# A gated delta-rule layer on one core: causal masks multiplied in on VectorE, in place of ScalarE copies and GpSimd masks

## The chip, the core and the metric

The kernel runs on one core of one Trainium2 chip. The metric is the device time of one execution in microseconds (us), as the median of several runs. The engines are named as the profile names them: PE is TensorE's matmul, PEld its weight load, DVE is VectorE, ACT is ScalarE, POOL is GpSimd, and SP is the engine that issues nearly all DMAs. Each engine works through its own instructions in a fixed order and stops at an instruction whose inputs are not there.

## The reference, cut to what matters

One layer (SEQ 2048, D_MODEL 1024) has an RWKV-7 time mixer with 12 heads of 64, a memory cross-attention beside it, an output projection and a squared-ReLU MLP. The time mixer's state update runs token by token:

```python
def step(S, inp):
    r_t, w_t, k_t, v_t, a_t, b_t = inp
    sa = jnp.einsum('bhvk,bhk->bhv', S, a_t)
    S = (S * w_t[:, :, None, :] + sa[..., None] * b_t[:, :, None, :]
         + v_t[..., None] * k_t[:, :, None, :])
    return S, jnp.einsum('bhvk,bhk->bhv', S, r_t)
```

Within a chunk of 64 tokens this becomes products of all tokens with all tokens (b and k against a and r), of which only the part with the source before the target token counts. For a that is strictly before, for r it includes the token itself. The masks of this case set the other part to zero.

## The kernel before

The program has three parts in time. First the input is normed and the first quarter of the input projection is made (0 to about 218 us). Then comes the scan: 16 pairs of two 64-token chunks, each with `prepare(p)`, `scan` and `post`, while the remaining projections, the memory attention and the output projection are laid between the scan's steps as filler (218 to about 1520 us). Last comes the MLP in four long stretches of matmuls (1520 us to the end).

The order on each engine is made by the framework's scheduler, from priorities: `dense` spreads the filler's steps over given stretches of pairs, and the first half of `prepare` is moved forward by `UPS = 400` ranks, so that it lies beside the scan of the pair before. The scheduler places each instruction where its own model of time lets it run, so an edit in one place moves instructions around it.

The change is in `prepare`, at the products within a chunk. For each chunk and each half `hb` of the heads, 6 matmuls (L390, shown as 12 in the profile, since each is two passes) write two PSUM tiles `pps` of 128x384. The tiles come from the pool `psa`, which has two buffers under the tag "a". So the next group of products can start only when both are copied out. The copies (L392) put them into the SBUF tile `PT`. Then two DMAs (L395) store the two 32x32 diagonal blocks to DRAM (`nd`). Ti is loaded from `nd` (L412), and a forward substitution of 46 + 46 dependent small DVE operations runs on it (`zt`, L431, and `Zw`, L435). Its result goes through DRAM (`zdr`) into `Z`; DVE transposes blocks of Z (`te`, L453), PE multiplies them with `PT` (L459), and the scan then uses `PT` and `Z` (L485 and on). The masks (L397, on GpSimd) work in place on `PT` behind the two stores: 64 rows by 12x64, then 64 rows by 12x128, for each chunk.

Other names below: `psco` (L772) are the memory attention's scores, `pout` (L629) the output projection, `wo` (L92 and L93) its weights split into a high and a low part, `sl` (L676) the token shift, `qt` (L756) the square of the memory attention's queries behind a load.

Of the kernel before, what the change touches and what calls it, by code (L numbers as in the profile page):

```python
# [13 lines left out]
ALU = mybir.AluOpType  # L14
# [5 lines left out]
P = 128  # L20
# [6 lines left out]
NB = MW // P  # L27
NH = 12
# [5 lines left out]
C = 64  # L34
# [26 lines left out]
def hybrid_layer(  # L61
# [6 lines left out]
    nc = tc.nc  # L68
# [129 lines left out]
    K = {}  # L198
# [82 lines left out]
    def prepare(p):  # L281
# [98 lines left out]
        for c in range(2):  # L380
            d = ch[c]
            d["PT"] = PT = ck.tile([P, NH, 2 * C], F32, name="PT", bufs=4)
            for hb in range(2):

                pps = [psa.tile([P, 3, 2 * C], F32, tag="a", name="pp") for _ in range(2)]
                for j in range(3):
                    b = 3 * hb + j
                    for q in range(2):
                        rs = slice(q * HD, q * HD + HD)
                        nc.tensor.matmul(pps[q][:, j, :], BK[c][rs, b, :], d["AR"][rs, b, :], start=True, stop=True)  # L390
                for q in range(2):
                    nc.scalar.copy(PT[:, q * NB + 3 * hb : q * NB + 3 * hb + 3, :], pps[q])  # L392
            for blk in range(2):
                bsl = slice(32 * blk, 32 * blk + 32)
                nc.sync.dma_start(nd[blk, c].rearrange("i s t -> s i t"), PT[bsl, :, bsl])  # L395
            for o, w in ((0, C), (C, 0)):
                nc.gpsimd.tensor_tensor(PT[o : o + C, :, w:], PT[o : o + C, :, w:],  # L397
                                        K["msk"][o : o + C, w:].unsqueeze(1).to_broadcast([C, NH, 2 * C - w]),
                                        op=ALU.mult)
        nc.vector.tensor_tensor(kp, kp, R, op=ALU.mult)  # L400
        psb = psz.tile([P, NH], F32, tag="z", name="psb")
        for b in range(NB):
# [24 lines left out]
        for s in range(31):  # L427
# [6 lines left out]
            for j0, j1 in parts:  # L434
                nc.vector.tensor_tensor(Zw[:, j0:j1, s + 1 :], Zw[:, j0:j1, s + 1 :], zt[:, j0:j1, :nt],  # L435
                                        op=ALU.add)
# [408 lines left out]
    S = scan_setup()  # L845
    rank["base"] = tc.cur_priority
    nxt = prepare(0)
    dense(*SPAN[0], (project(1), 184))
    dense(*SPAN[1], (mixed(project(2), memory(0), 184, 24), 208))
    dense(*SPAN[2], (mixed(project(3), memory(1, 2), 184, 48), 232))  # L850
    for p in range(NPAIR):
        d = nxt
        S, states = scan(d, S)
        if p + 1 < NPAIR:
            nxt = prepare(p + 1)
        post(p, d, states)
        if p == 3:
            dense(*SPAN[3], (mixed(output(0), memory(3), 64, 24), 88))
        elif p in (7, 11):
            dense(*SPAN[p // 4 + 3], (output(p // 4), 64))  # L860
        elif p in (13, 15):
            dense(*SPAN[p // 2], (output(3, (p // 2 % 2,)), 32))
# [104 lines left out]
    def layer1(hf, B):  # L967
# [14 lines left out]
        def w(src, name):  # L982
# [3 lines left out]
            return h, l  # L986

        nxt = prepare(0)
        for c in range(NCH):
            A, (S1, S2, S3, S4) = nxt  # L990
# [150 lines left out]
```

## Time and profile before

| what | value |
|---|---|
| median of 3 runs | 2778.41 us (2771.92 to 2782.58) |
| the profiled execution | 2781.47 us, of which its span is 2779.8 us |
| PE busy | 2620.1 us (94%), granted clock 0.956 on average |
| DVE, ACT, POOL busy | 1807.5, 1410.8, 413.1 us |

PE is busy for most of the span, so the time is read from PE: where it waits, and at which clock it works. The granted clock is a share of full speed; the chip grants 1.2 or 2.4 GHz, so 0.5 is the lower level and 1.0 the higher.

### The profile page before, as it was taken

The numbers are of one execution on the slowest core, as the hardware profiler recorded it, in microseconds if no ns is written. First come the engines' busy times: TensorE is split into PE (matmuls) and PEld (weight loads), VectorE is DVE, ScalarE is ACT, GpSimd is POOL, SyncE is SP. The second block draws the span as 40 slices with busy tenths as digits, with TensorE's granted clock in tenths as the row PEclk, the third lists the DMA queues.
The fourth block names the chain that finished last, engine by engine and source line by source line (L and its number), as shares of the span: only waits on it lengthen the run. The fifth ranks groups of instructions, "written<-read, shape, count | busy, mean of one in ns | idle before, by whom it ended". The sixth has DMA issues, their size and how long they took to land.

```text
span 2779.8 us, 49460 instructions
## 1 busy us (share of the span) xinstructions
PE 2620.1 (94%) x17620; PEld 2131.9 (77%) x17620; DVE 1807.5 (65%) x4500; ACT 1410.8 (51%) x3053; POOL 413.1 (15%) x236
## 2 busy tenths in 40 slices
PE   6989999999899998997996999999999999999999
PEld 4777777777677777777885888878888888888887
DVE  4556657676866666778568777765875666655564
ACT  5564456465645547363446444444744444544443
POOL 2002133425304241333111000000100000000000
PEclk9999999999989988798997999999999999999999
DMA  8987564665454544335574576786775444456675
GB/s 251 286 263 215 166 176 135 168 174 165 135 152 138 144 126 120 100 86 164 160 241 133 201 260 244 275 306 191 246 258 170 145 144 155 150 192 208 211 252 167
DMA packets 468444, 519.35 MB, mean 187 GB/s; under 512 B 117538, under 2 KB 291682, under 8 KB 468196
## 3 DMA queue, kind: packets, MB, share of 16 engines
q1 hardware_dynamic: 468196, 516.18, 60.0%
q8 instruction: 139, 2.28, 0.3%
q14 instruction: 109, 0.89, 0.1%
HBM read 361.86 MB, written 154.14 MB: 186 GB/s over the span
## 4 chain that ended last, share of the span: by engine, by line
PE 74%; DMA 10%; DVE 9%; ACT 2%; issue 2%; SPq 2%; POOL 1%; DVEq 0%; ACTq 0%; POOLq 0%
PE pu L964 23%; PE py L1073 22%; PE pz L102 12%; PE pout L629 5%; PE pp L390 2%; DVE zt L431 1%; DVE Zw L435 1%; DMA zdr<-Zw 1%; PE prhs L485 1%; DMA qt<-q_d 1%; DMA KT<-rk_d 1%; DMA Z<-zdr 1%; DMA xt<-in_x_dram 1%; DMA ws<-in_rw_in_dram 1%; PE py L522 1%
## 5 line engine op out<-in xcount | busy, mean ns | idle before, releaser
L102 PE MATMUL pz<-xh,w 128*128 128x512 f32 x1408 | 484.9, 413 | 4.5 <-DVE last L681 2.7
L1073 PE MATMUL py<-wpl,hhh 128*128 128x512 f32 x896 | 349.3, 390 | 0.0
L1073 PE MATMUL py<-wph,hhl 128*128 128x512 f32 x896 | 348.3, 389 | 0.0
L1073 PE MATMUL py<-wph,hhh 128*128 128x512 f32 x896 | 344.0, 391 | 0.0
L102 PEld LDWEIGHTS pz<-xh,w 128*128 128x128 f32 x1408 | 268.9, 193 | 71.8 <-issue 6.6
L93 DVE TENSOR_TENSOR hhl<-hr,hhh 128x512 fp32r<-128x512 f32 x224 | 154.7, 691 | 225.6 <-ACT hhh L92 225.5
L92 ACT CAST hhh<-hr 128x512 fp32r<-128x512 f32 x224 | 139.1, 621 | 311.1 <-PE py L1073 295.5
L102 PE MATMUL pz<-xl,w 128*128 128x512 f32 x704 | 287.7, 409 | 0.4 <-DVE xl L93 0.4
L629 PE MATMUL pout<-wo,xh 128*128 128x256 f32 x1024 | 218.7, 307 | 18.9 <-DVE wo L93 9.6
L431 DVE TENSOR_TENSOR zt<-Ti,Zw 96x96 f32<-96x96 f32 (+20 forms) x736 | 171.2, 256 | 69.3 <-DMA Ti<-nd 49.7
L397 POOL TENSOR_TENSOR PT<-PT,msk 64x768 f32<-64x768 f32 x64 | 178.6, 2790 | 131.4 <-ACT PT L392 129.1
L629 PEld LDWEIGHTS pout<-wo,xh 128*128 128x128 f32 x1024 | 174.5, 205 | 28.9 <-DVE wo L93 12.3
L1073 PEld LDWEIGHTS py<-wph,hhl 128*128 128x128 f32 x896 | 168.4, 188 | 35.0
L1073 PEld LDWEIGHTS py<-wph,hhh 128*128 128x128 f32 x896 | 168.4, 188 | 34.8 <-DVE u L999 0.2
L1073 PEld LDWEIGHTS py<-wpl,hhh 128*128 128x128 f32 x896 | 168.4, 188 | 34.6
L435 DVE TENSOR_TENSOR Zw<-Zw,zt 96x96 f32<-96x96 f32 (+20 forms) x736 | 161.2, 242 | 6.7
L102 PEld LDWEIGHTS pz<-xl,w 128*128 128x128 f32 x704 | 135.8, 193 | 29.8 <-issue 1.9
L93 DVE TENSOR_TENSOR wpl<-wr,wph 128x512 fp32r<-128x512 f32 x224 | 153.3, 684 | 3.8 <-ACT wph L92 3.8
L629 PE MATMUL pout<-wo,xl 128*128 128x256 f32 x512 | 153.1, 299 | 0.0
L86 POOL TENSOR_TENSOR nr<-nm,nhalf 128x1 f32<-128x1 f32 x34 | 28.1, 827 | 789.2 <-DVE nm L84 736.3
L92 ACT CAST wph<-wr 128x512 fp32r<-128x512 f32 x224 | 138.2, 617 | 8.5 <-PE pu L964 7.5
L390 PE MATMUL pp<-AR,BK 64*128 64x128 f32 x768 | 94.5, 322 | 18.5 <-ACT PT L392 16.3
(293 smaller groups left out, 5640.5 us busy)
## 6 DMA issues: line engine op xcount, KB each, us to landing
w<-w_d SPq DMA_DIRECT2D x264, 256.0 KB, 4.0
hr<-hc_d SPq DMA_DIRECT2D x224, 256.0 KB, 2.8
ws<-in_w_ff_dram SPq DMA_DIRECT2D x32, 1024.0 KB, 5.7
hc_d<-hs SPq DMA_DIRECT2D x128, 256.0 KB, 2.2
wr<-t_d SPq DMA_DIRECT2D x128, 256.0 KB, 3.1
wr<-in_w_ff_dram SPq DMA_DIRECT2D x96, 256.0 KB, 3.0
w_d<-w SPq DMA_DIRECT2D x88, 256.0 KB, 4.2
ws<-in_w_out_dram SPq DMA_DIRECT2D x80, 256.0 KB, 4.3
```

What stands on the lines that cost most here:

```text
L86: nc.gpsimd.tensor_tensor(t1, t0, nhalf[: ssum.shape[0], :n], op=ALU.pow)
L92: nc.scalar.copy(hi, src)
L93: nc.vector.tensor_tensor(lo, src, hi.bitcast(F32), op=ALU.subtract)
L102: nc.tensor.matmul(ps, a(k), b(k), start=(k == 0 and i == 0), stop=(k == nk - 1 and i == 2))
L390: nc.tensor.matmul(pps[q][:, j, :], BK[c][rs, b, :], d["AR"][rs, b, :], start=True, stop=True)
L397: nc.gpsimd.tensor_tensor(PT[o : o + C, :, w:], PT[o : o + C, :, w:], K["msk"][o : o + C, w:].unsqueeze(1).to_broadcast([C, NH, 2 * C - w] ...
L431: nc.vector.tensor_tensor(zt[:, j0:j1, :nt], Ti[:, s, s + 1 :].unsqueeze(1).to_broadcast([96, j1 - j0, nt]), Zw[:, j0:j1, s : s + 1].to_br ...
L435: nc.vector.tensor_tensor(Zw[:, j0:j1, s + 1 :], Zw[:, j0:j1, s + 1 :], zt[:, j0:j1, :nt], op=ALU.add)
L485: nc.tensor.matmul(pc[rs, h // 2, :], PT[:, head(h), :C], WV[:, h * HD : (h + 1) * HD], start=True, stop=True)
L629: nc.tensor.matmul(po[:, t, :], a(k, t), w[k][:, b], start=(k == 0 and i == 0 and t == 0), stop=(k == KB - 1 and i == 2 and t == 1))
L964: nc.tensor.matmul(ps, a[u][:, k * P : (k + 1) * P], b[v][:, k, :], start=(first and k == 0 and i == 0), stop=(k == 3 and i == 2), skip_gr ...
L1073: nc.tensor.matmul(ps[bk], a[u][:, m * P : (m + 1) * P], b[v], start=(fresh and c == 0 and t == 0), stop=(c == NCH - 1 and t == 2), skip_g ...
```

## The change

The ScalarE copy of each product tile becomes a VectorE multiplication with the mask, which reads the product from PSUM and the mask `msk` from SBUF and writes the masked product to `PT`. The two GpSimd operations per chunk go away. The stores to `nd` now carry masked blocks; the substitution reads only what lies above the diagonal.

```diff
                 for q in range(2):
-                    nc.scalar.copy(PT[:, q * NB + 3 * hb : q * NB + 3 * hb + 3, :], pps[q])
+                    nc.vector.tensor_tensor(PT[:, q * NB + 3 * hb : q * NB + 3 * hb + 3, :], pps[q],
+                                            K["msk"].unsqueeze(1).to_broadcast([P, 3, 2 * C]), op=ALU.mult)
             for blk in range(2):
                 bsl = slice(32 * blk, 32 * blk + 32)
                 nc.sync.dma_start(nd[blk, c].rearrange("i s t -> s i t"), PT[bsl, :, bsl])
-            for o, w in ((0, C), (C, 0)):
-                nc.gpsimd.tensor_tensor(PT[o : o + C, :, w:], PT[o : o + C, :, w:],
-                                        K["msk"][o : o + C, w:].unsqueeze(1).to_broadcast([C, NH, 2 * C - w]),
-                                        op=ALU.mult)
```

Lines behind the edit have numbers lower by 3 in the changed kernel (te is L453 before and L450 now).

The order on ACT before, at the products of the fourth pair: the copies to PT stand between other work, two of them behind `qt`, which waits for a load.

```order
L392 COPY PT<-pp 128x384 x2
L92 CAST xh<-pt 128x4x128 x3
L756 ACTIVATE qt<-qt 128x256
L392 COPY PT<-pp 128x384 x2
L92 CAST xh<-pt 128x4x128
L392 COPY PT<-pp 128x384
L150 ACTIVATE junk,nss<-xt 128x1024
L392 COPY PT<-pp 128x384 x2
L461 COPY te_2003<-pe 32x192
L470 COPY PT<-AR 64x6x64
L392 COPY PT<-pp 128x384
```

The order on DVE now, at the same place: the multiplications stand there, and six of the eight are behind the transposes `te` of the pair before, which wait for the load of Z.

```order
L84 TENSOR_SCALAR ym<-var 128x12
L392 TENSOR_TENSOR PT<-pp,msk 128x384
L349 SCALAR_TENSOR_TENSOR th_6823<-th_6845,kk 128x768
L392 TENSOR_TENSOR PT<-pp,msk 128x384
L450 STREAM_TRANSPOSE te<-Z_2000 32x192 x2
L539 SCALAR_TENSOR_TENSOR mean<-mean,yr 128x12
L350 SCALAR_TENSOR_TENSOR th_6823<-th_6823,EM 128x768
L365 TENSOR_TENSOR th_6845<-th_6845,KT 128x768
L673 SCALAR_TENSOR_TENSOR sl<-pz,muc,sl 128x511
L675 SCALAR_TENSOR_TENSOR sl<-last_149,muc,sl 128x1
L678 COPY last_150<-pz 128x1
L392 TENSOR_TENSOR PT<-pp,msk 128x384 x5
```

What moved: the emptying of the product tiles left ACT's row behind `qt` and entered DVE's row behind `te`.

The order on PE before, at the products of the last pair: all four groups stand one behind the other, with nothing between them.

```order
L522 MATMUL py_16310<-S,AR 64x64 x12
L528 MATMUL py_16310<-WV,PT 64x64 x12
L800 MATMUL po<-pT,vm 64x128 x7
L390 MATMUL pp<-AR,BK 128x128 x24
L629 MATMUL pout<-wo,xh 128x256 x3
L629 MATMUL pout<-wo,xl 128x256
```

And on PE now, from the first group of the same pair to the next rows: each group is followed by some 20 matmuls of the output projection.

```order
L390 MATMUL pp<-AR,BK 128x128 x6
L626 MATMUL pout<-wo,xh 128x256
L626 MATMUL pout<-wo,xl 128x256 x2
L626 MATMUL pout<-wo,xh 128x256 x2
L626 MATMUL pout<-wo,xl 128x256
L626 MATMUL pout<-wo,xh 128x256 x2
```

What moved: filler now lies between the groups of the last pair.

## Rows read from the trace of the kernel before

**Rows 1.** The page's busy time of each engine (share of the span, instructions).

```profile
PE 2620.1 (94%) x17620; PEld 2131.9 (77%) x17620; DVE 1807.5 (65%) x4500; ACT 1410.8 (51%) x3053; POOL 413.1 (15%) x236
```

**Rows 2.** Two stretches: length, busy by engine, clock, DMA share, GB/s.

```profile
218.00:1520.00 1302.00, 1193.65 (x11377) 971.88 (x11375) 879.66 (x2887) 684.86 (x1708) 382.72 (x191) 0.92 0.54 154
1520.00:2780.00 1260.00, 1249.72 (x5438) 1017.96 (x5438) 809.45 (x1282) 598.56 (x1027) 9.93 (x7) 0.99 0.63 208
```

**Rows 3.** Waits of PE, 218:1520: us in total, times, longest.

```profile
PE pt L936 <- DVE xn L931: 21.8, 5, 8.0
PE pp L390 <- ACT PT L392: 16.3, 7, 4.6
PE pout L629 <- DVE wo L93: 9.6, 7, 2.8
PE psco L772 <- DVE sl L676: 9.2, 1, 9.2
```

**Rows 4.** Groups, 218:1420: count, busy us, mean ns, idle before, releasers.

```profile
L397 POOL TENSOR_TENSOR PT<-PT,msk 64x768 f32<-64x768 f32 x64 | 178.6, 2790 | 131.4 <-ACT PT L392 129.1
...
L390 PE MATMUL pp<-AR,BK 64*128 64x128 f32 x768 | 94.5, 322 | 18.5 <-ACT PT L392 16.3 <-DVE BK L368 1.8 <-DVE BK L360 0.2
...
L392 ACT COPY PT<-pp 128x384 f32<-128x384 f32 x128 | 56.7, 479 | 80.8 <-PE pp L390 80.4
...
L459 PE MATMUL pe<-te,PT 32*32 32x32 f32 x768 | 38.1, 197 | 10.1 <-ACT te L461 5.6 <-DVE te L453 3.7 <-ACT BKT L419 0.7
```

**Rows 5.** Timeline of DVE, 749:764: start us, us, instruction.

```profile
750.70 1.89 DVE L435 TENSOR_TENSOR Zw<-Zw,zt 96x96 f32<-96x96 f32 x1
752.62 3.53 DVE L431 TENSOR_TENSOR zt<-Ti,Zw 96x88 f32<-96x88 f32 x1
...
758.09 1.72 DVE L431 TENSOR_TENSOR zt<-Ti,Zw 96x80 f32<-96x80 f32 x1
759.85 3.46 DVE L435 TENSOR_TENSOR Zw<-Zw,zt 96x80 f32<-96x80 f32 x1
763.34 0.23 DVE L431 TENSOR_TENSOR zt<-Ti,Zw 96x72 f32<-96x72 f32 x1
```

**Rows 6.** Timeline of POOL, 749:764; x2 is two masks merged.

```profile
749.74 6.30 POOL L397 TENSOR_TENSOR PT<-PT,msk 64x768 f32<-64x768 f32 x2
...
757.91 5.30 POOL L397 TENSOR_TENSOR PT<-PT,msk 64x768 f32<-64x768 f32 x2
```

**Rows 7.** Timeline of PE, 757:768; in brackets the idle time before.

```profile
767.37 1.22 PE L772 MATMUL psco<-kTm,qt 64*128 64x256 f32 x2 [9.21 <-DVE sl L676]
```

**Rows 8.** Timeline of DVE, 1270:1277.

```profile
1271.37 3.55 DVE L93 TENSOR_TENSOR wo<-ws,wo 128x256 fp32r<-128x256 f32 x1
...
1275.88 0.41 DVE L93 TENSOR_TENSOR wo<-ws,wo 128x256 fp32r<-128x256 f32 x1
```

**Rows 9.** Timeline of POOL, 1263:1277.

```profile
1264.14 10.49 POOL L397 TENSOR_TENSOR PT<-PT,msk 64x768 f32<-64x768 f32 x2 [23.65 <-ACT PT L392]
```

**Rows 10.** Timeline of PE, 1266:1277.

```profile
1274.98 0.58 PE L629 MATMUL pout<-wo,xh 128*128 128x256 f32 x1 [2.79 <-DVE wo L93]
```

**Rows 11.** All 32 of line 565: shortest, median, longest in ns.

```profile
L565 DVE TENSOR_TENSOR mixT<-mixT,pg x32: 529/547/556, 366.3 to 1419.5; 128x384 f32<-128x384 f32 x32
```

**Rows 12.** Two stretches, columns as in rows 2.

```profile
772.00:796.00 24.00, 23.52 (x190) 17.86 (x189) 15.05 (x69) 12.23 (x34) 1.47 (x1) 0.72 0.64 172
...
1274.00:1291.00 17.00, 14.23 (x95) 13.82 (x95) 16.26 (x20) 3.96 (x10) 16.11 (x8) 0.82 0.30 100
```

**Rows 13.** Timeline of ACT, 412:425.

```profile
416.89 0.42 ACT L756 ACTIVATE qt<-qt 128x256 f32<-128x256 f32 x1 [3.21 <-DMA qt<-q_d]
417.21 0.84 ACT L392 COPY PT<-pp 128x384 f32<-128x384 f32 x2
```

**Rows 14.** Timeline of PE, 412:425.

```profile
417.72 3.86 PE L390 MATMUL pp<-AR,BK 64*128 64x128 f32 x18 [3.17 <-ACT PT L392]
```

**Rows 15.** Waits of DVE, 218:1520: us in total, times, longest.

```profile
DVE te L453 <- DMA Z<-zdr: 51.6, 21, 7.1
```

## The prediction

> **What bounds the kernel now.** I read the busy times first: PE works for 94% of the span, DVE for 65%, ACT for 51%, POOL for 15% [rows 1]. A share over the whole span says little, so the second view cuts it at the end of the scan. In the MLP, from 1520 us on, PE is busy 1249.72 of 1260 us at a granted clock of 0.99; nothing that the change touches runs there, and it stays as it is. In the scan, from 218 to 1520 us, PE is busy 1193.65 of 1302 us at 0.92 [rows 2]. So PE bounds this stretch too, and what can be won is its idle time, 1302 - 1193.65 = 108.4 us, and the lower clock. DVE is busy there for 879.66 us (68%) and ACT for 684.86 us (53%): neither is the bound by its sum.
>
> The third view says what ends PE's idle time [rows 3]. The largest item, 21.8 us before the transposes at L936, lies at the MLP's start and waits for DVE's norm; the change leaves it. The second, 16.3 us in 7 waits, is the product group of L390 waiting for ACT's copies of PT, which the change removes. The next two, 9.6 and 9.2 us, wait for DVE, and the question is why DVE was late there.
>
> **The change part by part.**
>
> *ACT loses 128 copies* of 479 ns, 56.7 us busy [rows 4]. Since ACT is idle for nearly half of the scan, the busy time itself is worth nothing to the end; what counts is the wait behind it, costed below.
>
> *POOL loses 64 masks*, 178.6 us busy [rows 4]. PE doesn't wait for POOL at these places: the masked part of PT is needed only by the scan, after the substitution and its way through DRAM. So as work they are worth nothing either. But they cost DVE. Around 750 us, two pairs of masks run on POOL [rows 6], and beside them four small operations of the substitution take 1.89, 3.53, 1.72 and 3.46 us, while the next one, of 72 elements after one of 80, takes 0.23 us [rows 5]. Each ends when a mask ends. Taking 0.23 us as the due time of each, DVE loses 1.66 + 3.30 + 1.49 + 3.23 = 9.7 us. Behind them in DVE's order is the token shift `sl`, for whose PSUM buffer the matmul `psco` waits: PE is idle for 9.21 us [rows 7]. Without the masks that wait is gone: 9.2 us. At 1271.37 us the same happens to a split of the output weights: 3.55 us instead of 0.41 [rows 8], ending with the mask of 1264.14 + 10.49 = 1274.63 us [rows 9] give or take 0.3, and PE waits 2.79 us for it [rows 10]. Together PE gets back 9.2 + 2.8 = **12.0 us**. Bounds: nothing, if the work in front of those matmuls is late for another reason after the move; upwards, all of the 9.6 us in rows 3 instead of 2.8 is 18.8 us.
>
> On this the Trainium skill has a rule, in SBUF — State Buffer, Who interferes with whom: a VectorE instruction with two inputs in SBUF and a GpSimd instruction that reads SBUF exclude each other for the whole instruction, whichever comes first, and one with at most one SBUF input is not touched. The durations just read agree. By the rule every overlap of that kind, not only these five, holds up DVE, which makes a rival below.
>
> *DVE gains 128 multiplications.* The nearest row is a product of the same size with one input in PSUM and one in SBUF, the gate of L565: 547 ns, and none of 32 over 556 [rows 11], though five POOL operations per pair run beside DVE there. So 128 x 0.547 = 70.0 us more, less what the masks held up (9.7 + 3.1 us read here; it can't be more than the masks' own 178.6 us). With the smaller of these, 57 us more in a stretch where DVE is idle for 422 us: it goes to about 72%, and stays off the bound by its sum.
>
> *The wait of the products moves from ACT to DVE.* PE is idle for 18.5 us before L390 [rows 4]. The reason is order, not speed: at 417 us two copies stand behind `qt`, which waits 3.21 us for a load, and PE then waits 3.17 us [rows 13, 14]. That goes, but on DVE the multiplications stand behind other things. In 12 of the 15 later pairs at least one is placed behind a `te` of the pair before, as the order above shows for the fourth. `te` waits 51.6 us in 21 waits for Z [rows 15], so what is late next is DVE at `te`, then PT, then the next product group on PE. Bounds: 0, as PE has 10 to 25 filler matmuls between most groups, and 51.6 us, if each of those waits reaches PE. The nearest row is the other matmul that follows directly on `te`: L459, idle for 10.1 us [rows 4]. That small number beside 51.6 says that PE is mostly behind DVE at this point and doesn't feel the wait. I take 10.1. The multiplication is also 547 - 479 = 68 ns longer than the copy; over 7 waits of two tiles this is 1.0 us (8.7 us if all 128 were on the path). Sum: -18.5 + 10.1 + 1.0 = **-7.4 us**, between -18.5 and +41.8.
>
> *The clock.* After the wait of 9.21 us the granted clock fell, and the stretch from 772 to 796 us ran at 0.72; the one from 1274 to 1291, after the waits at the weights, at 0.82 [rows 12]. In time at full speed that is 24 x 0.28 = 6.7 and 17 x 0.18 = 3.1 us. If PE waits less there, this comes back; but the new order has waits of its own elsewhere. I take half, **-4.9 us**, of 0 to -9.8.
>
> *Stores and order.* The DMAs of L395 are the same and wait for DVE now, 0.14 us later per half. The substitution behind them, 46 + 46 operations per pair, starts that much later, hidden by the filler; without filler it would be 16 x 0.3 = 4.8 us. PE's filler moves a little between pairs, as at the last one, where it now covers the products.
>
> The sum is -12.0 - 7.4 - 4.9 = -24.3 us. Against the profiled execution's 2781.47 us this is 2757.2. That execution is 3.1 us over the median of the runs shown, so the median becomes 2778.4 - 24.3 = **2754 us**.
>
> **Rivals.**
>
> *The wait only moves (same).* For it: the order on DVE, and the 51.6 us. Suppose that each of the 12 pairs hands PE one wait of 51.6 / 21 = 2.46 us: 29.5 us in place of 18.5, with 1.0 for the longer operation. With the 12.0 us of the masks this is 12.0 - 12.0 = 0, and the clock gives nothing: 2778 us. Against it: L459's 10.1 us.
>
> *DVE becomes the late engine (slower).* One mechanism: all of the 51.6 us at `te` reach PE through the two product buffers, since both are full and the copies to empty them stand behind `te`. Then -18.5 + 51.6 + 1.0 - 12.0 = +22.1 us: 2800 us. It decides from 18.5 + 12.0 - 1.0 = 29.5 us of new wait on; above it the kernel is slower. For it: before, a late DVE held up only DVE here, and now it holds up PE. Against it: the filler between the groups.
>
> *The masks held up more than I could follow (faster still).* As a mechanism of this kernel: POOL's masks lengthen DVE's substitution in most pairs, and later work on DVE with it, so that all of PE's waits for DVE in rows 3 at `wo` and `sl` (18.8 us), all 18.5 us before L390 and all 9.8 us of the clock go: 47 us, 2731 us. This is what the Trainium skill's rule on the two engines, named above, would make of it. For it: the masks' 178.6 us are long beside the operations of 0.2 us that they can hold up. Against it: PE doesn't wait for DVE in most pairs.
>
> *It does nothing.* PE's waits are set by DMAs and the scheduler's order, and new ones come for old ones: 2778 us, give or take 10.
>
> **How the numbers follow.** My forecast (gain of 14 to 35 us) gets 0.41, the larger gain 0.12, the moved wait and no effect together 0.28 with a spread of 10 us about 2778, slower 0.19. About 0.5%, 14 us, is what a measurement of this kernel can tell from no change. Faster by more than that: 0.41 + 0.12 = 0.53, and the same 0.28, slower 0.19. The range reaches from the larger gain, 2733, to the middle of no change and the slower case, 2789, which leaves out about 0.2. The forecast's own range is 2743 to 2764.
>
> **What would show it.** Right: the substitution's operations keep to 0.2 to 0.4 us except beside POOL's remaining five operations per pair; the multiplication takes about 0.55 us; PE's idle time before L390 is 8 to 15 us and its releaser is DVE's PT; PE's idle time from 218 to 1520 us falls from 108 to about 88 us; the granted clock there is 0.92 or a little over. Wrong: idle time before L390 of over 30 us, with `te` and its wait for Z in front of PT; or long DVE operations that stay although the masks are gone; or a lower clock with the same idle time, from an order that spreads PE's work in another way.

## The result, and the profile after

The changed kernel takes 2745.16 us (median of 6 runs, 2736.0 to 2752.87), the kernel before 2776.57 us in 6 runs (2771.92 to 2782.58). The ratio is 0.9874, with a 95% interval of 0.9851 to 0.9897: 31.4 us less, inside the stated range of 2733 to 2789 us, where 2754 us and a gain of 24.3 us were forecast. The profiled execution took 2744.66 us, 36.8 us less than the one of before; its span is 2742.9 us.

The page's busy times of the changed kernel answer to [rows 1].

```profile
PE 2610.6 (95%) x17620; PEld 2128.4 (78%) x17620; DVE 1811.1 (66%) x4628; ACT 1353.9 (49%) x2925; POOL 235.9 (9%) x172
```

ACT has lost 56.9 us and POOL 177.2 us, the copies and the masks. DVE has 128 instructions more, of 0.55 us each, and yet only 3.6 us more of busy time: its other work has become shorter by some 65 us.

Next the stretches of the changed kernel, cut at its MLP's first matmul (columns as in [rows 2]).

```profile
218.00:1484.70 1266.70, 1183.30 (x11336) 968.20 (x11334) 882.16 (x3013) 626.06 (x1569) 205.29 (x127) 0.93 0.56 157
1484.70:2742.90 1258.20, 1249.70 (x5440) 1017.90 (x5440) 809.88 (x1283) 598.14 (x1031) 10.21 (x8) 1.00 0.63 209
```

The same cut of the kernel before, at its MLP's first matmul, gives this row.

```profile
218.00:1518.00 1300.00, 1192.43 (x11375) 971.38 (x11373) 877.93 (x2885) 682.86 (x1705) 382.49 (x191) 0.92 0.54 154
```

The stretch is 33.3 us shorter, and nearly all of the gain is there; the MLP gave the other 3.6 us. PE's idle time in the stretch was 1300 - 1192.43 = 107.6 us and is 83.4 us now, a fall of 24.2 us, and PE's busy time has fallen by 9.1 us, at a granted clock of 0.93 in place of 0.92. A little of this is a shift: 39 more of the matmuls run ahead of 218 us now. From the start of the program to the MLP, with 12180 matmuls in both kernels, PE's busy time fell from 1369.19 to 1360.87 us, by 8.3 us, and its idle time by 25.0 us.

What ends PE's idle time in the changed kernel, from 218 to 1485 us, answers to [rows 3].

```profile
PE pt L933 <- DVE xn L928: 22.4, 5, 8.8
PE pp L390 <- DVE PT L392: 15.0, 9, 3.3
PE pout L626 <- ACT wo L92: 7.3, 4, 2.7
PE pe L456 <- DVE te L450: 5.6, 5, 1.5
PE pb L415 <- ACT BKT L416: 4.6, 1, 4.6
PE pout L626 <- DVE wo L93: 4.0, 4, 1.5
```

The single wait of 9.2 us at `psco` is gone, and the one for DVE's `wo` fell from 9.6 to 4.0 us. But the wait ahead of the products is still there: it has changed its releaser from ACT's PT, 16.3 us, to DVE's PT, 15.0 us.

Two groups of the same stretch answer to [rows 4].

```profile
L390 PE MATMUL pp<-AR,BK 64*128 64x128 f32 x756 | 103.5, 321 | 17.2 <-DVE PT L392 15.0 <-DVE BK L368 2.0
...
L392 DVE TENSOR_TENSOR PT<-pp,msk 128x384 f32<-128x384 f32 x128 | 67.9, 548 | 62.4 <-PE pp L390 62.1
```

The new operation takes 548 ns, the 547 ns of [rows 11]. Its shortest, median and longest, and those of the substitution's `zt`, read as follows in the answers on lines 392 and 428 of the changed kernel.

```profile
L392 DVE TENSOR_TENSOR PT<-pp,msk x128: 505/547/558, 221.1 to 1260.3; 128x384 f32<-128x384 f32 x128
```

```profile
L428 DVE TENSOR_TENSOR zt<-Ti,Zw x736: 157/205/1806, 247.5 to 1297.7; 96x126 f32<-96x126 f32 x16, 96x96 f32<-96x96 f32 x16, 96x31 f32<-96x31 f32 x8, 96x58 f32<-96x58 f32 x8
```

No `zt` takes 3.5 us any more. What is left stands beside POOL's other operations, as the timelines of DVE and of POOL at 967 us show: four operations of 8 to 32 elements take 1.34 to 1.69 us, and each ends within 0.05 us of an operation of `post` on POOL.

```profile
967.55 1.38 DVE L428 TENSOR_TENSOR zt<-Ti,Zw 96x32 f32<-96x32 f32 x1
...
969.18 1.34 DVE L428 TENSOR_TENSOR zt<-Ti,Zw 96x24 f32<-96x24 f32 x1
...
970.77 1.69 DVE L428 TENSOR_TENSOR zt<-Ti,Zw 96x16 f32<-96x16 f32 x1
...
972.71 1.66 DVE L428 TENSOR_TENSOR zt<-Ti,Zw 96x8 f32<-96x8 f32 x1
```

```profile
967.41 1.47 POOL L540 TENSOR_TENSOR yc<-yc,yr 128x768 f32<-128x768 f32 x1
968.96 1.52 POOL L541 TENSOR_TENSOR yc<-yc,mean 128x768 f32<-128x768 f32 x1
970.56 1.87 POOL L542 TENSOR_TENSOR yc<-yc,lgr 128x768 f32<-128x768 f32 x1
972.51 1.82 POOL L545 TENSOR_TENSOR yc<-yc,Vn 128x768 f32<-128x768 f32 x1
```

### The profile page after: what moved, and what is told of

Same layout as the page of the kernel before. It is cut to its first block, busy times and chain, and to the rows that moved or that the text cites. A ratio compares the mean times of both kernels' runs of the same rounds, so it can differ in the third digit from the quotient of the medians.

```text
span 2742.9 us, 49338 instructions
## 1 busy us (share of the span) xinstructions
PE 2610.6 (95%) x17620; PEld 2128.4 (78%) x17620; DVE 1811.1 (66%) x4628; ACT 1353.9 (49%) x2925; POOL 235.9 (9%) x172
## 4 chain that ended last, share of the span: by engine, by line
PE 64%; DVE 5%; DMA 4%; ACT 1%; issue 1%; SPq 1%; POOL 0%; DVEq 0%; ACTq 0%; POOLq 0%
PE pu L961 23%; PE py L1070 22%; PE pz L102 5%; PE pout L626 4%; DMA ws<-in_w_out_dram 1%; PE pp L390 1%; DVE zt L428 1%; PE prhs L482 1%; DVE wo L93 1%; PE psco L769 1%; PE pe L463 1%; PE pw L488 1%; PE pe L456 1%; PE pS L495 1%; DVE Zw L432 1%
## 5 line engine op out<-in xcount | busy, mean ns | idle before, releaser
L428 DVE TENSOR_TENSOR zt<-Ti,Zw 96x96 f32<-96x96 f32 (+20 forms) x736 | 154.2, 232 | 72.0 <-DMA Ti<-nd 50.7
L432 DVE TENSOR_TENSOR Zw<-Zw,zt 96x96 f32<-96x96 f32 (+20 forms) x736 | 150.3, 227 | 6.5 <-DVE zt L428 0.2
L390 PE MATMUL pp<-AR,BK 64*128 64x128 f32 x768 | 104.4, 320 | 17.2 <-DVE PT L392 15.0
L390 PEld LDWEIGHTS pp<-AR,BK 64*128 64x128 f32 x768 | 85.6, 214 | 36.3 <-DVE PT L392 18.5
L392 DVE TENSOR_TENSOR PT<-pp,msk 128x384 f32<-128x384 f32 x128 | 67.9, 548 | 62.4 <-PE pp L390 62.1
```

The lines of the kernel that those rows point to most:

```text
L392: nc.vector.tensor_tensor(PT[:, q * NB + 3 * hb : q * NB + 3 * hb + 3, :], pps[q], K["msk"].unsqueeze(1).to_broadcast([P, 3, 2 * C]), op=A ...
L428: nc.vector.tensor_tensor(zt[:, j0:j1, :nt], Ti[:, s, s + 1 :].unsqueeze(1).to_broadcast([96, j1 - j0, nt]), Zw[:, j0:j1, s : s + 1].to_br ...
```

## The experiments

The theory, H: the gain comes from GpSimd's masks no longer holding up VectorE. Rival A: it comes from ScalarE losing the copies. Rival Q: it comes from GpSimd's own queue, in which short operations for the norms stood behind masks. A fourth possibility is that the scheduler's order happened to come out better. Ratios are to the kernel before on the same chip, with 95% intervals.

### Masks and copies apart

The first run keeps the masks on GpSimd in the changed kernel, so that POOL works as before.

```diff
                 nc.sync.dma_start(nd[blk, c].rearrange("i s t -> s i t"), PT[bsl, :, bsl])
+            for o, w in ((0, C), (C, 0)):
+                nc.gpsimd.tensor_tensor(PT[o : o + C, :, w:], PT[o : o + C, :, w:], ...
```

> The changed kernel, with the GpSimd masks kept in place behind the stores (masking twice gives the same values). Theory H (the gain comes from GpSimd's masks no longer holding up VectorE's operations with two inputs in SBUF): the gain goes, 2770 to 2800 us, and small operations of the substitution take 1.8 to 3.5 us again. Rival A (the gain comes from ScalarE's copies and their waits leaving ScalarE, and from the order that follows): the time stays within 8 us of the changed kernel's 2745 us. Rival Q (the gain comes from GpSimd's own queue: its short operations for the norms no longer wait behind masks): 2765 to 2780 us, as under H.

Measured: 2778.48 us, ratio 0.9985 (0.997 to 1.0001). The gain is gone, as H and Q expected and A did not. The timelines of this kernel's DVE and POOL around 1280 us show the long operations again: 3.56 and 3.51 us, which end with masks. Between them stands a small comparison: a multiplication out of PSUM (L392) runs beside an operation of `post` on POOL and takes its usual 0.54 us, while the next `zt`, with both inputs in SBUF, takes 1.37 us and ends with that operation.

```profile
1279.47 3.56 DVE L436 TENSOR_TENSOR Zw<-Zw,zt 96x96 f32<-96x96 f32 x1
...
1283.79 0.23 DVE L436 TENSOR_TENSOR Zw<-Zw,zt 96x88 f32<-96x88 f32 x1
...
1285.56 0.54 DVE L392 TENSOR_TENSOR PT<-pp,msk 128x384 f32<-128x384 f32 x1
1286.03 1.37 DVE L432 TENSOR_TENSOR zt<-Ti,Zw 96x80 f32<-96x80 f32 x1
...
1293.23 3.51 DVE L432 TENSOR_TENSOR zt<-Ti,Zw 96x40 f32<-96x40 f32 x1
```

```profile
1277.38 5.53 POOL L398 TENSOR_TENSOR PT<-PT,msk 64x768 f32<-64x768 f32 x2 [0.24 <-DVE mean L543]
...
1285.43 1.87 POOL L546 TENSOR_TENSOR yc<-yc,lgr 128x768 f32<-128x768 f32 x1
1291.08 5.59 POOL L398 TENSOR_TENSOR PT<-PT,msk 64x768 f32<-64x768 f32 x2 [3.78 <-DVE PT L392]
```

The stretch up to this kernel's first MLP matmul gives the hold on VectorE as a whole.

```profile
218.00:1516.40 1298.40, 1188.76 (x11375) 969.27 (x11374) 927.45 (x3013) 630.37 (x1577) 383.08 (x191) 0.92 0.55 154
```

The same 3013 operations keep DVE busy for 927.45 us, 45.3 us more than in the changed kernel, and PE is idle for 109.6 us in place of 83.4.

The second run is the other half: the copies stay on ScalarE, and the masks are left out, so that this kernel's products are not masked at all.

```diff
-            for o, w in ((0, C), (C, 0)):
-                nc.gpsimd.tensor_tensor(PT[o : o + C, :, w:], PT[o : o + C, :, w:], ...
```

> The kernel before, with ScalarE's copies as they were and the masks left out altogether, so its output lacks the causal masks within a chunk. H: the whole gain or more without touching the copies, 2735 to 2755 us, and PE's idle time ahead of the products stays near 18 us with ScalarE's PT as releaser. Rival A: no gain, 2770 to 2780 us. Rival Q: as under H.

Measured: 2742.53 us, ratio 0.9854 (0.9835 to 0.9874). The whole gain is there with ScalarE's copies untouched. PE's idle time ahead of the products is shorter than expected, and its releaser is ScalarE's PT (waits of this kernel's PE, 218 to 1487 us).

```profile
PE pout L625 <- ACT wo L92: 20.5, 5, 9.1
PE pe L455 <- DVE te L449: 12.6, 6, 3.5
PE pp L390 <- ACT PT L392: 12.1, 7, 6.0
```

Here too DVE's busy time fell without any change to its own work, from 877.93 us in the kernel before to 812.23 us, by 65.7 us.

```profile
218.00:1486.10 1268.10, 1175.47 (x11363) 960.12 (x11361) 812.23 (x2885) 679.16 (x1697) 203.06 (x127) 0.93 0.56 157
```

So the two parts of the change can be read from four kernels:

| | masks on GpSimd | no masks on GpSimd |
|---|---|---|
| copies on ScalarE | 1 (before) | 0.9854 (no masks at all) |
| products leave PSUM on VectorE | 0.9985 | 0.9874 (the change) |

Taking the masks off GpSimd is worth 1.1% with VectorE emptying PSUM and 1.5% with ScalarE. Moving the emptying is worth 0.15% in one row and costs 0.2% in the other, which is nothing within the intervals. Rival A falls. That the gain comes from the masks leaving GpSimd is shown; whether it comes by way of VectorE (H) or of GpSimd's queue (Q) is the next question.

The third run asks whether the masks are better on VectorE even as separate operations in SBUF.

```diff
-                nc.gpsimd.tensor_tensor(PT[o : o + C, :, w:], PT[o : o + C, :, w:],
+                nc.vector.tensor_tensor(PT[o : o + C, :, w:], PT[o : o + C, :, w:],
```

> The kernel before, with ScalarE's copies as they were and the same two masks per chunk in place, on VectorE in place of GpSimd: 64 operations of 768 and 1536 elements with two inputs in SBUF, about 32 x (0.95 + 1.75) = 86 us of VectorE. H: still a gain, 2745 to 2768 us, since VectorE takes less time for them than it lost. Rival A: none or a loss, 2775 to 2800 us.

Measured: 2759.31 us, ratio 0.9914 (0.9895 to 0.9933), in the range that H expected, but not for the reason given. The 64 masks take VectorE 100.6 us, more than the 65.7 us that it lost while GpSimd made them, and its busy time up to the MLP is 924.65 us against 877.93 in the kernel before. VectorE works longer and the kernel is faster, so VectorE's sum is not what PE pays for. Rival Q would expect a gain here too, as GpSimd's queue is free of the masks; this run does not separate it from H. Multiplying on the way out of PSUM is better (0.9874), with VectorE busy for 882.16 us.

```profile
L397 DVE TENSOR_TENSOR PT<-PT,msk 64x768 f32<-64x768 f32 x64 | 100.6, 1572 | 33.8 <-ACT PT L392 33.2
```

### GpSimd's queue as full, without reading

The next run fills GpSimd's queue in the changed kernel with memsets, which write SBUF and read nothing, behind one short operation per chunk that waits for PT. The priority is set back after them, so that the rest keeps its ranks.

```diff
+        K["scr"] = cb.tile([P, 128], F32, name="scr")
...
+            kept = tc.cur_priority
+            nc.gpsimd.tensor_tensor(K["scr"][:, :1], PT[:, NH - 1, :1], K["msk"][:, :1], op=ALU.mult)
+            for _ in range(24):
+                nc.gpsimd.memset(K["scr"], 0.0)
+            tc.cur_priority = kept
```

> The changed kernel, and on GpSimd, for each chunk, one short operation that waits for PT and then 24 memsets of 128x128 (0.2 us each, about 5 us together, as long as the two masks were) that only write a scratch tile. GpSimd's queue is as full as before the change, but its added work reads nothing from SBUF. H: no loss, 2740 to 2755 us. Rival Q: the gain goes, 2765 to 2780 us. Rival A: 2740 to 2755 us as under H.

Measured: 2768.8 us, ratio 0.9951 (0.9923 to 0.998). The time misses H's range and lies in that of rival Q. By the ratio, against the kernel before on the same chip (2782.16 us), neither fits whole: of the 1.11% that the kept masks cost, the memsets cost 0.77%. They took 160.1 us on POOL, where the masks took 178.6. The stretch up to this kernel's first MLP matmul reads:

```profile
218.00:1508.00 1290.00, 1203.02 (x11365) 977.32 (x11363) 878.91 (x3013) 629.95 (x1570) 369.23 (x927) 0.92 0.55 155
```

PE's idle time is 87.0 us, 3.6 more than in the changed kernel, and DVE's busy time, 878.91 us, is even a little less than that kernel's 882.16: VectorE isn't held up. The loss lies in PE's busy time, 1203.02 us in place of 1183.30; from the start to the MLP, with the same 12180 matmuls, it is 1380.58 us in place of 1360.87. The order of this kernel differs too, and the same was run again in another order, UPS = 380.

> The changed kernel with the write-only memsets on GpSimd, in the order of UPS = 380, to be read against the changed kernel in that order (ratio 0.983 to the kernel before). H: PE's idle time ahead of the MLP stays near 77 us, as VectorE isn't held; ratio 0.980 to 0.990, with what the order does. Rival Q (GpSimd's queue matters): the loss of the first memset run, about 0.8%, comes again: 0.988 to 0.994, with PE's idle time up.

Measured: 2750.98 us, ratio 0.9895 (0.9873 to 0.9918), against 0.983 for the changed kernel in that order (below): a loss of 0.65%. The ratio lies in both ranges, but the sign that was to separate them went against H: PE's idle time did not stay near 77 us, it rose to 1274.6 - 1180.99 = 93.6 us from 76.8. DVE's busy time, 877.57 us, is again not longer than in the changed kernel, as the stretches of that kernel and of this one in the order of UPS = 380 show.

```profile
218.00:1471.70 1253.70, 1176.86 (x11337) 959.70 (x11337) 886.66 (x3013) 627.65 (x1569) 203.89 (x127) 0.93 0.56 159
```

```profile
218.00:1492.60 1274.60, 1180.99 (x11367) 957.94 (x11363) 877.57 (x3013) 631.32 (x1575) 365.06 (x927) 0.94 0.56 157
```

The masks kept in this order cost more:

> The changed kernel with the GpSimd masks kept in place, in the order of UPS = 380. H and Q: the gain goes, ratio 0.996 to 1.008. Rival A: 0.980 to 0.988.

Measured: 2782.92 us, ratio 1.0014 (1.0 to 1.0027), a loss of 1.84% against 0.983. So of what GpSimd's masks cost, write-only work of nearly the same length costs 69% in one order and 35% in the other; these shares are rough, since each ratio has an interval of 0.1 to 0.3% either way. That the whole gain comes from the hold on VectorE is thus not shown; whether the rest is GpSimd's queue or what 25 more instructions per chunk do to the order, the two runs don't tell.

The traces speak against the queue, without settling it. If short operations of GpSimd had come late behind masks, waits that end with them should shrink when the masks go. The longest of these waits in the kernel before, and the same one without the masks (218 to 1500 us), did not.

```profile
DVE mean L542 <- POOL yr L86: 8.7, 7, 2.4
```

```profile
DVE mean L538 <- POOL yr L86: 10.3, 8, 2.4
```

With the products leaving PSUM on VectorE it is 6.0 us with the masks and 4.5 us without. These are a few us beside a gain of 31 to 41.

### Is it the order?

```diff
-UPS = 400
+UPS = 380        (and 420)
```

> A control of the order: the kernel before, with UPS = 380 in place of 400, which moves the first half of each prepare by 20 ranks and so reorders instructions on all engines without taking anything away. H: within 10 us of the kernel before, as the masks stay on GpSimd. If the gain of the change is an accident of the scheduler's order, such a move gives or takes as much as the change did, some 30 us.

Measured: 2786.94 us, ratio 1.0013 (1.0 to 1.0027).

> The same control with UPS = 420 on the kernel before. H: within 10 us of it. Accident of the order: up to 30 us either way.

Measured: 2806.16 us, ratio 1.008 (1.0053 to 1.0108): 23.4 us slower, from the order alone, where H expected at most 10 us.

> The same control with UPS = 380 on the changed kernel. H: still faster than the kernel before by 20 to 40 us. Accident of the order: the gain goes, or the spread over the two controls is as large as the gain.

Measured: 2732.26 us, ratio 0.983 (0.9806 to 0.9854), the fastest of all kernels here; it beats the changed kernel's 0.9874. It is 50.5 us faster than the kernel before on that chip, more than the 20 to 40 us that H expected.

> The same control with UPS = 420 on the changed kernel. H: still faster than the kernel before by 20 to 40 us. Accident of the order: the gain goes.

Measured: 2753.12 us, ratio 0.9896 (0.9874 to 0.9919), 29.7 us faster, as expected.

In each order the changed kernel is faster than the kernel before: by 1.83% at 380 (0.983 / 1.0013), by 1.26% at 400, by 1.82% at 420 (0.9896 / 1.008). The order alone moves the kernel before by up to 0.8% and the changed one by up to 0.7% (0.983 to 0.9896). So the gain is no accident, but its size depends on the order by half a per cent.

### VectorE held up by nothing

The last two runs carry H further: the five large operations of `post` go to VectorE as well.

```diff
-        nc.gpsimd.tensor_tensor(yc, yc, bc(rstd), op=ALU.mult)
+        nc.vector.tensor_tensor(yc, yc, bc(rstd), op=ALU.mult)
...
```

> The changed kernel in the order of UPS = 380, with the five remaining large operations of post (128x768, two inputs in SBUF) moved from GpSimd to VectorE as well: 80 operations of about 0.95 us, 76 us of VectorE more, while GpSimd keeps only its short ones. H: the long holds on VectorE, some 50 us, nearly go, so VectorE gains 26 us net of work and the time is 2715 to 2740 us, ratio 0.976 to 0.986. If VectorE's load is what counts: slower than without, ratio 0.985 to 0.995.

Measured: 2753.5 us, ratio 0.9907 (0.9883 to 0.9931), slower than without the move (0.983).

> The same move of the five operations at UPS = 400, the order of the changed kernel (ratio 0.987). H: ratio 0.978 to 0.990. If VectorE's load is what counts: 0.990 to 1.0.

Measured: 2760.24 us, ratio 0.9926 (0.9904 to 0.9949), slower than the changed kernel (0.9874). The expectation of H failed in both, and the other one, that VectorE's load is what counts, gave ranges that hold. The holds are gone, as line 428 shows in the first of the two:

```profile
L428 DVE TENSOR_TENSOR zt<-Ti,Zw x736: 153/205/300, 249.2 to 1309.2; 96x126 f32<-96x126 f32 x16, 96x96 f32<-96x96 f32 x16, 96x31 f32<-96x31 f32 x8, 96x58 f32<-96x58 f32 x8
```

The longest `zt` is 300 ns. The 80 operations moved, at 948 to 954 ns each in this kernel, add 76 us to VectorE's work, and its busy time up to the MLP grew by 18.0 us only, from 886.66 to 904.68 us, so some 58 us of holds went. Still, PE's idle time grew by 8.3 us, to 85.2 us, and its busy time by 9.9 us.

```profile
218.00:1489.90 1271.90, 1186.73 (x11374) 968.88 (x11372) 904.68 (x3093) 631.92 (x1574) 67.73 (x47) 0.93 0.56 157
```

The waits of its PE from 218 to 1490 us are these.

```profile
PE pout L626 <- ACT wo L92: 14.6, 6, 5.3
PE pp L390 <- DVE BK L368: 9.5, 2, 9.0
PE pp L390 <- DVE PT L392: 6.5, 6, 2.4
```

The same waits without the move, in the order of UPS = 380, read as follows.

```profile
PE pp L390 <- DVE PT L392: 9.7, 9, 2.2
PE pout L626 <- ACT wo L92: 9.2, 4, 3.7
PE pp L390 <- DVE BK L368: 7.5, 3, 5.0
```

So the products' own input BK, which DVE makes, was late here without the move too, and the move added 2.0 us; the wait for ScalarE's `wo` grew by 5.4 us. In the order of UPS = 400 the wait for BK did grow, from 2.0 us to this one in the second run:

```profile
PE pp L390 <- DVE BK L368: 10.8, 1, 10.8
```

That VectorE's work of `post` makes BK late is a reading of this one wait, and no run tested it. What costs the time when `post` moves stays open.

## Why the prediction was right

*What bounds the kernel*: right. PE's idle time from 218 us to the MLP was the place, 24.2 us of the 33.3 us gained there, and the rest is PE's own busy time, 8.3 us of it for the same matmuls, at a little higher clock.

*POOL's masks hold up DVE, 12.0 us for PE*: that the masks hold up DVE and that the time goes with them was right, and the term was too small. `psco` lost its 9.2 us and `wo` 5.6 us against the 2.8 taken [rows 3, 10]. But these two waits are not a fixed price of the masks: in the run that kept the masks behind the multiplications, `psco` does not wait and `wo` for 0.5 us, and the whole time is back in other waits. The masks as a whole were worth 1.1 to 1.8% in the pairs of runs above, 31 to 51 us. The stretches that I read, 9.7 + 3.1 us of holds, were a small part of the whole: DVE's busy time in the stretch rose by 4.2 us with 67.9 us of new work, so some 64 us of other work went, and the pairs of runs with the same DVE work give 65.7 and 45.3 us. That a part of the loss, 35% in one order and 69% in the other, comes back with POOL work that only writes was not foreseen, and how much of the gain goes by way of VectorE stays open.

*DVE gains 128 multiplications, and stays off the bound by its sum*: right in the duration, 548 ns, and in the sum, 70% of the stretch against the 72% forecast.

*The wait of the products moves from ACT to DVE, -7.4 us*: this term was wrong in size. PE's idle time before L390 fell by 1.3 us, from 18.5 to 17.2 [rows 4], not by 7.4; it lies above the 8 to 15 us that I named as the sign of being right. The 2 x 2 table says the same of the time: the move is worth nothing. The nearest row that I took, L459's 10.1 us, was not the price of standing behind `te`: that matmul now waits 8.1 us, and `te` itself waits 40.9 us for Z in place of 51.6, but the products wait 15.0 us for DVE's PT where they waited 16.3 us for ACT's. The order on DVE that stands ahead of the prediction is the third pair's, by the trace (344 to 370 us); in the fourth (414 to 428 us), four of the eight multiplications stand behind `te`, not six.

*The clock, -4.9 us*: PE's busy time fell by 9.1 us, or by 8.3 us for the same matmuls. The size is of the kind that was allowed (up to 9.8), and the memset run shows how loose this term is: 1380.58 and 1360.87 us from the start to the MLP for the same 12180 matmuls in two orders.

*The rivals.* That the wait only moves was right as to the wait, and wrong as to the time, because the masks' part paid. DVE as the late engine didn't come. The larger gain was nearer than I thought: 31.4 us measured, between the forecast's 24 and its 47.

The errors had opposite signs. Of the 33.3 us by which the MLP starts earlier, 8.3 are PE's busy time (4.9 forecast), 1.3 the products' wait (7.4 forecast), and the remaining 33.3 - 8.3 - 1.3 = 23.7 us other idle time of PE (12.0 forecast): 6.1 us too much in the one term, 15.1 us too little in the other two. That the sum came within some 7 us of the measured gain is luck in part.

## What to carry to other kernels

Before moving work between engines, look at what it holds up while it runs, not only at its own busy time: small operations on VectorE whose longest is ten times their median, each ending with a GpSimd operation, are such a sign. GpSimd's share of 15%, with no wait in the profile that ended with its masks, hid a cost of over 1%. And where a scheduler sets the order, run the same edit in two or three orders: here the order alone was worth up to 0.8%, and an edit that gains less than that can't be judged from one of them.

## What was not expected of the hardware

VectorE's multiplication with one input in PSUM took 505 to 558 ns in all 128 cases, and 541 to 559 ns in the run that kept GpSimd's masks beside it, while operations of VectorE with both inputs in SBUF, 0.2 us otherwise, took up to 3.5 us beside the masks. This is as the Trainium skill says in SBUF — State Buffer, Who interferes with whom: a VectorE instruction with two inputs in SBUF contends with a GpSimd instruction that reads SBUF, and one with at most one such input, outside the modes that use two ports, does not. The runs add that giving VectorE the whole work of the masks in SBUF (0.9914) is cheaper than letting GpSimd do it beside VectorE. GpSimd work that only writes SBUF did not lengthen DVE's busy time (878.91 us against 882.16), and still cost 0.65 to 0.77%; why is open.
